# Final RMSNorm of a transformer layer: the last multiplies of the second half-rows on GpSimd instead of VectorE

## The chip, the core and the metric

The kernel runs on one core of a Trainium2 chip. A core has five engines with a queue each, worked off in order: TensorE (PE in the profile; its weight loads are PEld), VectorE (DVE), ScalarE (ACT), GpSimd (POOL) and SyncE (SP), which here issues all DMAs. They wait for each other through semaphores. The metric is the device time of one execution in microseconds, the median of the runs shown.

## The reference

One encoder layer over two batches with the same weights, 1024 and 512 rows of width 1024, then a last norm. What matters here is the end of it:

```python
def _rmsnorm(x, g):
    xf = x.astype(jnp.float32)
    y = xf * lax.rsqrt(jnp.mean(xf * xf, axis=-1, keepdims=True) + EPS)
    return (y * g.astype(jnp.float32)).astype(x.dtype)
...
    h = _rmsnorm(x, g_ffn)
    x = x + (jax.nn.silu(h @ w_ffn_gate) * (h @ w_ffn_up)) @ w_ffn_down
...
    return _rmsnorm(x, g_final)
```

## The kernel before

The 1536 rows are 12 tiles of 128 rows (t = 0 to 11), in two groups of six: g = 0 holds tiles 0 to 5, g = 1 tiles 6 to 11. The mixers run first, up to about 750 us. Then the feed-forward part loops over group, eleven slices p of the hidden width, and w = 0 (gate) or 1 (up). Each (g, p, w) is one `ffn_set`: seven products of 12 matmuls each on TensorE into three PSUM tiles psX, psY and psZ (products 0, 2, 4 and 6 use psX, 1 uses psY, 3 and 5 use psZ). A product that adds on to a PSUM tile waits until ScalarE has copied the sum so far out of it (`cp`, L1091). Every operand is a float32 split in a high and a low part, by a cast on ScalarE (L981) and a subtraction on VectorE (L982). After the gate set of the next slice, `down` multiplies the activations with the down weights into psd (L1156), and VectorE adds psd to the tile's row x2[t] (L1158), in the order 1, 3, 5, 0, 2, 4 within a group.

The last norm of a tile stands in two functions. `fin_ss` takes a buffer `out` (yo in the profile), squares the two halves of x2[t] into it on ScalarE with the row sums as a by-product (L1129), and makes the row's factor r on GpSimd in three instructions on 128x1 values: L1131, L1132 and the power of -0.5, L1133. `fin_y` multiplies: each half of the row is one instruction on VectorE (L1142), (x2 times r) times gF, 128x512, and then one DMA of 256 KB from SP (L1143). Here x2, yo and the gain gF all lie in SBUF.

This happens in two places. Tiles 0 to 5 are finished in the first gate set of g = 1, while its matmuls run; this is called the middle stage below, 1350 to 1400 us. Tiles 6 to 11 are finished in the last `down`, the end stage, from 1837 us on. The buffers yo come from the pool `wr` of four buffers of 4 KB per partition, which also holds the raw gate and up weights; so a yo, or a weight load, can take a buffer only when the output DMAs of the yo before it have landed. The sums of squares sq0 and sq1 have one buffer each, so the squares of the next tile wait for L1131 and L1132 of this one.

Matmuls keep the order in which they are written. On the other engines a scheduler sets the order of the queues, and which free buffer a tile takes, from its own cost model; so an edit in one place can change the queues of all four around it.

Of the kernel before, what the change touches and what calls it, by code (L numbers as in the profile page):

```python
# [13 lines left out]
ALU = mybir.AluOpType  # L14
# [787 lines left out]
def of_phase(tc, hp, x, catT, g_ffn, wg, wu, wd, g_fin, y, ident, before, hc, x2d):  # L802

    nc = tc.nc
    V, A, G, PE = nc.vector, nc.scalar, nc.gpsimd, nc.tensor
# [6 lines left out]
    x2 = {i: xr_p.tile([128, D], F32, tag=f"x{i}", name=f"x2_{i}") for i in range(2)}  # L812
# [309 lines left out]
    def fin_ss(t, keep=1):  # L1122
        out = wr.tile([128, D], F32, tag="raw", name="yo")
        sq = [small.tile([128, 1], F32, tag=f"sq{j}", bufs=1, name=f"sq{j}") for j in range(2)]
        ss = small.tile([128, 1], F32, tag="ss", name="ss")
        r = small.tile([128, 1], F32, tag="rf", bufs=4, name="rs")
        for j in range(2):
            js = slice(j * 512, (j + 1) * 512)
            A.activation(out[:, js], x2[t][:, js], AF.Square, accum_out=sq[j])  # L1129
            if j == 0:  # L1130
                G.tensor_scalar(ss, sq[0], 1.0, EPS * D, op0=ALU.mult, op1=ALU.add)  # L1131
        G.tensor_scalar(ss, sq[1], ss, 1.0 / D, op0=ALU.add, op1=ALU.mult)  # L1132
        G.tensor_tensor(r, ss, mh, op=ALU.pow)  # L1133
        fin.append((t, out, r))
        if len(fin) > keep:
            fin_y()

    def fin_y():
        t, out, r = fin.pop(0)
        for j in range(2):  # L1140
            js = slice(j * 512, (j + 1) * 512)
            V.scalar_tensor_tensor(out[:, js], x2[t][:, js], r, gF[0][:, js], op0=ALU.mult, op1=ALU.mult)  # L1142
            nc.sync.dma_start(y[t * 128:(t + 1) * 128, js], out[:, js])  # L1143

    def down(g, p):
# [20 lines left out]
    gF = [None]  # L1166
    LAST = 2 * NP - 1
    ends = (1, 3, 5, 0, 2, 4)

    def slots(n):  # L1170
        g, p, w = seq[n]
        z = [[] for _ in range(7)]
        if n == 0:
            z[0].append(lambda: o_tr(10))
            z[1].append(lambda: o_tr(11))
            z[2] += [lambda: fetch(1), lambda: fetch(2)]
        for i in range(4):
            z[i + 2 if n == 0 else i + 1 if n == LAST + 1 else i].append(lambda i=i: load_a(n + 1, i))
        if w == 1:
            for i in range(2):  # L1180
                z[i if n == len(seq) - 1 else 2 * i + 2].append(lambda i=i: load_d(p, i))
        if n == LAST:
            for ci in range(6):
                z[ci + 1].append(lambda ci=ci: load_sum(1, ci))
        if n == LAST + 1:
            z[2] += [load_gf, lambda: down(0, NP - 1)]
            for i, o in enumerate(ends):
                z[3 + i // 2].append(lambda o=o: fin_ss(o))
            z[6].append(fin_y)
        if n == LAST + 2:  # L1190
            for i, o in enumerate(ends):
                z[i].append(lambda o=o: reload(o))
        return z
# [16 lines left out]
    while fin:  # L1210
        fin_y()
# [121 lines left out]
```

## Time and profile before

| | |
|---|---|
| median of three runs | 1869.37 us (1869.08 to 1870.72) |
| the profiled execution | 1866.71 us |
| its span, first to last instruction | 1864.9 us |
| TensorE busy, share of the span | 98% |
| VectorE busy | 64% |
| ScalarE busy | 46% |
| GpSimd busy | 12% |
| mean granted TensorE clock | 0.997 |

The profile is of one execution; its span is 1.8 us shorter than its device time, and that is 2.7 us under the median. Busy shares are of the whole span; a stage of 50 us has its own.

### The profile page before, as it was taken

What the parts mean: (1) busy time and instruction counts of PE and PEld (TensorE: products, weight loads), DVE (VectorE), ACT (ScalarE), POOL (GpSimd) and SP (SyncE); (2) the same over time, 40 slices, a digit from 0 to 9 for tenths busy, and PEclk for the clock granted to TensorE, in tenths of its full rate; (3) what the DMA queues carried; (4) which work ended last, traced back from release to release, by engine and by line L of the source; (5) the groups of instructions that cost most, each with busy time, mean ns of one, the idle gap of its engine ahead of it and who ended that gap; (6) DMA issues with size and microseconds to landing.
All of it is one profiled execution on the core that took longest, in us unless ns stands there. A gap on an engine that the chain in (4) does not pass through costs nothing.

```text
span 1864.9 us, 28927 instructions
## 1 busy us (share of the span) xinstructions
PE 1822.6 (98%) x10734; PEld 1647.4 (88%) x10734; DVE 1196.0 (64%) x2389; ACT 853.0 (46%) x1882; POOL 215.9 (12%) x425
## 2 busy tenths in 40 slices
PE   8999999999999999998999999999999999999997
PEld 7889898898788878888999999999899999999996
DVE  6754555556756574548666666666887666666655
ACT  7764555556666663425333333333453333333332
POOL 4322212122322221000000000000010000000001
PEclk9999999999999999999999999999999999999999
DMA  7422022132222254366222222222462222222202
GB/s 251 133 88 88 19 69 60 58 102 83 76 84 76 61 175 141 97 183 220 70 76 69 68 72 75 69 68 68 132 226 94 69 68 68 69 68 68 69 23 91
DMA packets 113581, 174.67 MB, mean 94 GB/s; under 512 B 11017, under 2 KB 79497, under 8 KB 113441
## 3 DMA queue, kind: packets, MB, share of 16 engines
q1 hardware_dynamic: 113440, 172.83, 29.7%
q8 instruction: 84, 1.38, 0.3%
q14 instruction: 57, 0.46, 0.1%
HBM read 144.69 MB, written 28.05 MB: 93 GB/s over the span
## 4 chain that ended last, share of the span: by engine, by line
PE 76%; issue 8%; DVE 5%; DMA 5%; ACT 4%; POOL 1%; SPq 0%; POOLq 0%; DVEq 0%; ACTq 0%
PE psd L1156 18%; PE psX L1067 18%; PE pj L717 17%; PE psZ L1067 9%; PE psY L1067 4%; PE ptr L402 1%; DMA wraw<-in_w_in 1%; DMA bq<-hc 1%; PE pso L832 1%; PE psc L373 1%; PE psc L377 1%; PE pgl L541 1%; DVE wl L217 1%; ACT wh L216 1%; PE pv L473 1%
## 5 line engine op out<-in xcount | busy, mean ns | idle before, releaser
L717 PE MATMUL pj<-wh,hh 128*128 128x384 f32 (+1 forms) x768 | 284.4, 370 | 0.7 <-ACT wh L216 0.7
L717 PE MATMUL pj<-wl,hh 128*128 128x384 f32 (+1 forms) x768 | 260.6, 339 | 0.2 <-DVE wl L217 0.2
L717 PE MATMUL pj<-wh,hl 128*128 128x384 f32 (+1 forms) x768 | 260.4, 339 | 0.1
L1158 DVE TENSOR_TENSOR x<-psd,x 128x512 f32<-128x512 f32 x264 | 181.3, 689 | 111.1 <-PE psd L1156 111.0
L1156 PE MATMUL psd<-dh,ah 128*128 128x512 f32 x528 | 205.8, 390 | 1.4 <-DVE x L1158 1.4
L1156 PE MATMUL psd<-dl,ah 128*128 128x512 f32 x528 | 206.0, 390 | 0.1
L1156 PE MATMUL psd<-dh,al 128*128 128x512 f32 x528 | 206.0, 390 | 0.0
L981 ACT CAST dh<-wdr 128x1024 fp32r<-128x1024 f32 x44 | 46.4, 1055 | 306.6 <-PE psd L1156 295.9
L982 DVE TENSOR_TENSOR fl<-raw,fh 128x1024 fp32r<-128x1024 f32 x132 | 161.0, 1221 | 39.5 <-ACT fh L981 39.4
L981 ACT CAST fh<-raw 128x1024 fp32r<-128x1024 f32 x132 | 138.7, 1052 | 99.4 <-PE psX L1067 52.5
L717 PEld LDWEIGHTS pj<-wh,hh 128*128 128x128 f32 x768 | 145.2, 189 | 23.0 <-issue 14.8
L717 PEld LDWEIGHTS pj<-wl,hh 128*128 128x128 f32 x768 | 145.5, 189 | 2.0 <-DVE wl L217 1.0
L717 PEld LDWEIGHTS pj<-wh,hl 128*128 128x128 f32 x768 | 144.6, 188 | 0.7 <-DVE hl L177 0.4
L1131 POOL TENSOR_SCALAR ss<-sq 128x1 f32<-128x1 f32 x12 | 4.6, 382 | 990.9 <-ACT yo L1129 990.9
L1156 PEld LDWEIGHTS psd<-dh,ah 128*128 128x128 f32 x528 | 99.1, 188 | 22.5 <-DVE x L1158 2.3
L1156 PEld LDWEIGHTS psd<-dh,al 128*128 128x128 f32 x528 | 99.1, 188 | 20.9 <-DVE al L982 0.3
L1156 PEld LDWEIGHTS psd<-dl,ah 128*128 128x128 f32 x528 | 99.1, 188 | 20.6 <-DVE dl L982 0.5
L217 DVE SCALAR_TENSOR_TENSOR wl<-wraw,gm,wh 128x384 fp32r<-128x384 f32 (+1 forms) x128 | 79.7, 644 | 19.1 <-ACT wh L216 18.4
L362 POOL TENSOR_SCALAR sc<-sc,mx 128x512 f32<-128x512 f32 x96 | 66.5, 695 | 178.6 <-DVE mx L361 164.7
L216 ACT ACTIVATE wh<-wraw,gm 128x384 fp32r<-128x384 f32 (+1 forms) x128 | 75.8, 618 | 21.8 <-DMA wraw<-in_w_in 19.6
L360 ACT ACTIVATE sc<-sc,mx 128x512 f32<-128x512 f32 x96 | 68.8, 717 | 23.8 <-DVE mx L359 22.3
L1091 ACT COPY s<-psX 128x384 f32<-128x384 f32 x88 | 41.8, 475 | 48.3 <-PE psX L1067 48.3
(282 smaller groups left out, 4426.5 us busy)
## 6 DMA issues: line engine op xcount, KB each, us to landing
raw<-in_w_gate SPq DMA_DIRECT2D x44, 512.0 KB, 3.8
raw<-in_w_up SPq DMA_DIRECT2D x44, 512.0 KB, 3.7
wdr<-in_w_down SPq DMA_DIRECT2D x44, 512.0 KB, 4.0
wraw<-in_w_in SPq DMA_DIRECT2D x112, 192.0 KB, 2.5
bq<-hc SPq DMA_DIRECT2D x18, 384.0 KB, 3.6
hc<-hst SPq DMA_DIRECT2D x24, 256.0 KB, 5.0
out_y<-yo SPq DMA_DIRECT2D x24, 256.0 KB, 2.0
craw<-catT SPq DMA_DIRECT2D x11, 512.0 KB, 3.8
```

The lines of the kernel that those rows point to most:

```text
L216: A.activation(h[:, :n], r[:, :n], AF.Copy, scale=gm[:, k:k + 1])
L217: V.scalar_tensor_tensor(l[:, :n], r[:, :n], gm[:, k:k + 1], f32(h)[:, :n], op0=ALU.mult, op1=ALU.subtract)
L360: A.activation(sc[:, :w], sc[:, :w], AF.Exp, bias=nm, scale=0.125, accum_out=l)
L362: G.tensor_scalar(sc[:, :w], sc[:, :w], rl, 1.0, op0=ALU.mult, op1=ALU.mult)
L373: PE.matmul(ps[h][:, 0:256], lhsT=qf[r, 128 * t:128 * t + 128], rhs=strided(kf[r, 32 * t:32 * t + 1], (32, 2), (288, 4), (1, 32)), start=T ...
L717: PE.matmul(ps[:, :cols], lhsT=l_[:, k, :], rhs=r_[:, :cols], start=(k == 0 and i == 0), stop=(k == 7 and i == 2))
L981: A.copy(h, r)
L982: V.tensor_tensor(l, r, f32(h), op=ALU.subtract)
L1067: PE.matmul(ps, lhsT=a_[:, sl], rhs=b_[kk // 2][:, kk % 2], start=(first and kk == 0 and j == 0), stop=(kk == 3 and j == 2), skip_group_ch ...
L1091: A.copy(s, ps)
L1156: PE.matmul(ps, lhsT=a_[:, sl], rhs=b_[:, js], start=(i == 0 and q == 0), stop=(i == 1 and q == 2))
L1158: V.tensor_tensor(xs, ps, xs, op=ALU.add)
```

## The change

In `fin_y`, the second half of each row (j = 1) goes to GpSimd as two instructions, x2 times r into yo and yo times gF in place, for all tiles but t = 10, the last one in the order of the end stage. The first half of each row, and both halves of tile 10, stay one instruction on VectorE. The DMAs stay on SP.

```diff
         for j in range(2):
             js = slice(j * 512, (j + 1) * 512)
-            V.scalar_tensor_tensor(out[:, js], x2[t][:, js], r, gF[0][:, js], op0=ALU.mult, op1=ALU.mult)
+            if j and t != 6 + ends[-1]:
+                G.tensor_scalar(out[:, js], x2[t][:, js], r, 1.0, op0=ALU.mult, op1=ALU.mult)
+                G.tensor_tensor(out[:, js], out[:, js], gF[0][:, js], op=ALU.mult)
+            else:
+                V.scalar_tensor_tensor(out[:, js], x2[t][:, js], r, gF[0][:, js], op0=ALU.mult, op1=ALU.mult)
             nc.sync.dma_start(y[t * 128:(t + 1) * 128, js], out[:, js])
```

The new lines are L1143 and L1144; VectorE's multiply becomes L1146, and later lines move by four (L1156 is L1160, L1158 is L1162). `ends` is (1, 3, 5, 0, 2, 4).

The scheduler's order moves with it. First GpSimd in the end stage, tiles 8 and 10 (x2_8 is tile 8; ss and rs are the small values, numbers are those of buffers). Before:

```order
L1131 TENSOR_SCALAR ss_18770<-sq0_18768 128x1
L1132 TENSOR_SCALAR ss_18770<-sq1_18769,ss_18770 128x1
L1133 TENSOR_TENSOR rs_18771<-ss_18770,mh2_9258 128x1
L1131 TENSOR_SCALAR ss_18800<-sq0_18798 128x1
L1132 TENSOR_SCALAR ss_18800<-sq1_18799,ss_18800 128x1
L1133 TENSOR_TENSOR rs_18801<-ss_18800,mh2_9258 128x1
```

And now:

```order
L1131 TENSOR_SCALAR ss_18778<-sq0_18776 128x1
L1132 TENSOR_SCALAR ss_18778<-sq1_18777,ss_18778 128x1
L1133 TENSOR_TENSOR rs_18779<-ss_18778,mh2_9258 128x1
L1143 TENSOR_SCALAR yo_18775<-x2_8_14861,rs_18779 128x512
L1144 TENSOR_TENSOR yo_18775<-yo_18775,gF_18643 128x512
L1131 TENSOR_SCALAR ss_18809<-sq0_18807 128x1
L1132 TENSOR_SCALAR ss_18809<-sq1_18808,ss_18809 128x1
L1133 TENSOR_TENSOR rs_18810<-ss_18809,mh2_9258 128x1
```

So the two large multiplies of a tile stand ahead of the next tile's three small instructions. The same holds for every tile of both stages but one (in the middle, tile 0's L1131 slips between the two multiplies of tile 5).

Then ScalarE in the middle stage, around the copies out of psX and psZ (yo_14655 is tile 0's buffer, yo_14684 tile 2's and yo_14698 tile 4's; the names DMAHW are the semaphores of DMAs). Before:

```order
L1091 COPY s_14749<-psX_14734 128x384 [waits PE_49]
L1129 ACTIVATE yo_14655,sq0_14656<-x2_0_8985 128x512 [waits DMAHW3_49,DMAHW4_49,DVE_49,Pool_49]
L1129 ACTIVATE yo_14655,sq1_14657<-x2_0_8985 128x512 [waits Pool_49]
L1129 ACTIVATE yo_14684,sq0_14685<-x2_2_9261 128x512 [waits DMAHW5_49,DMAHW6_49,DVE_49,Pool_49]
L1129 ACTIVATE yo_14684,sq1_14686<-x2_2_9261 128x512 [waits Pool_49]
L1091 COPY s_14797<-psX_14734 128x384 [waits PE_49]
L981 CAST ah_14771<-s_14749 128x384 [waits DVE_49]
L1091 COPY s_14823<-psZ_14736 128x384 [waits PE_49]
L1129 ACTIVATE yo_14698,sq0_14699<-x2_4_9278 128x512 [waits DMAHW2_49,DMAHW1_49,Pool_49]
L1129 ACTIVATE yo_14698,sq1_14700<-x2_4_9278 128x512 [waits Pool_49]
```

And now (yo_14687 is tile 2's, yo_14702 tile 4's):

```order
L1091 COPY s_14755<-psX_14740 128x384 [waits PE_49]
L1129 ACTIVATE yo_14687,sq0_14688<-x2_2_9261 128x512 [waits DMAHW6_49,DVE_49,DMAHW7_49,Activation_49,Pool_49]
L1129 ACTIVATE yo_14687,sq1_14689<-x2_2_9261 128x512 [waits Pool_49]
L1129 ACTIVATE yo_14702,sq0_14703<-x2_4_9278 128x512 [waits DMAHW0_49,DMAHW1_49,DVE_49,Pool_49]
L1129 ACTIVATE yo_14702,sq1_14704<-x2_4_9278 128x512 [waits Pool_49]
L981 CAST ah_14777<-s_14755 128x384 [waits DVE_49]
L1091 COPY s_14803<-psX_14740 128x384 [waits PE_49]
L981 CAST fh_14805<-raw_14420 128x1024 [waits DVE_49]
L1091 COPY s_14829<-psZ_14742 128x384 [waits PE_49]
```

The squares of tile 4 now stand ahead of the second copy out of psX and of the copy out of psZ. Read with the whole program, the DMAs waited for are the outputs of the tile that had the buffer: tile 3's squares wait for the outputs of tile 1 (as before), tile 5's for those of tile 3, tile 2's for those of tile 5, and tile 4's for those of tile 0; tile 0's wait for none. Before, tile 5's waited for none, tile 0's for tile 3, tile 2's for tile 5, tile 4's for tile 0.

## Rows read from the trace of the kernel before

**Rows 1.** Page, part 1: busy us, share of the span, instructions, by engine.

```profile
PE 1822.6 (98%) x10734; PEld 1647.4 (88%) x10734; DVE 1196.0 (64%) x2389; ACT 853.0 (46%) x1882; POOL 215.9 (12%) x425
```

**Rows 2.** All waits of PE, 1300 to 1866: total us, times, longest.

```profile
PE psX L1067 <- ACT s L1091: 1.5, 1, 1.5
PE psd L1156 <- DVE x L1158: 1.4, 2, 1.0
PE psZ L1067 <- ACT s L1091: 0.5, 1, 0.5
```

**Rows 3.** Chain that ended last, 1336 to 1440: start us, us, what.

```profile
1358.33 0.67 DVE yo L1142
1359.02 2.43 DMA out_y<-yo
...
1361.79 1.33 ACT yo L1129 x4
...
1367.87 2.60 DMA out_y<-yo
...
1370.58 1.35 ACT yo L1129 x4
...
1372.57 0.56 POOL rs L1133
...
1375.49 0.47 ACT s L1091
...
1378.30 1.43 DVE yo L1142 x2
...
1380.18 5.38 DMA raw<-in_w_up
```

**Rows 4.** Timeline, end stage, TensorE, VectorE and GpSimd: start us, us, engine, line, operation.

```profile
1853.94 0.39 PE L1156 MATMUL psd<-dh,al 128*128 128x512 f32 x1
...
1857.80 0.68 DVE L1158 TENSOR_TENSOR x<-psd,x 128x512 f32<-128x512 f32 x1
...
1860.40 1.41 DVE L1142 SCALAR_TENSOR_TENSOR yo<-x,rs,gF 128x512 f32<-128x512 f32 x2 [1.26 <-POOL rs L1133]
...
1842.80 0.55 POOL L1133 TENSOR_TENSOR rs<-ss,mh 128x1 f32<-128x1 f32 x1
...
1859.47 0.26 POOL L1132 TENSOR_SCALAR ss<-sq,ss 128x1 f32<-128x1 f32 x1 [1.54 <-ACT yo L1129]
1859.82 0.55 POOL L1133 TENSOR_TENSOR rs<-ss,mh 128x1 f32<-128x1 f32 x1
```

**Rows 5.** Groups of GpSimd: count, busy us, mean ns, idle before.

```profile
L362 POOL TENSOR_SCALAR sc<-sc,mx 128x512 f32<-128x512 f32 x96 | 66.5, 695 | 178.6 <-DVE mx L361 164.7 <-DVE mx L359 13.1
...
L582 POOL TENSOR_TENSOR gr<-gr,zt 128x512 f32<-128x512 f32 x12 | 15.4, 1285 | 42.1 <-ACT zt L581 42.1
```

**Rows 6.** Timeline where GpSimd and VectorE overlap; L217's durations, min/median/max ns.

```profile
1841.22 0.19 POOL L1131 TENSOR_SCALAR ss<-sq 128x1 f32<-128x1 f32 x1 [462.96 <-ACT yo L1129]
...
1854.10 0.57 POOL L1131 TENSOR_SCALAR ss<-sq 128x1 f32<-128x1 f32 x1 [0.27 <-ACT yo L1129]
...
1853.86 0.75 DVE L1142 SCALAR_TENSOR_TENSOR yo<-x,rs,gF 128x512 f32<-128x512 f32 x1 [0.66 <-POOL rs L1133]
...
55.37 1.29 POOL L255 TENSOR_TENSOR lat<-zt,lat 128x512 fp32r<-128x512 f32 x1 [0.68 <-PE pj L717]
...
55.46 1.62 DVE L217 SCALAR_TENSOR_TENSOR wl<-wraw,gm,wh 128x384 fp32r<-128x384 f32 x1
...
L217 DVE SCALAR_TENSOR_TENSOR wl<-wraw,gm,wh x128: 596/616/1618, 5.5 to 654.9; 128x384 fp32r<-128x384 f32 x112, 128x416 fp32r<-128x416 f32 x16
```

**Rows 7.** Timeline, middle stage, GpSimd and TensorE.

```profile
1352.47 0.55 POOL L1133 TENSOR_TENSOR rs<-ss,mh 128x1 f32<-128x1 f32 x1
...
1373.28 0.33 PE L1067 MATMUL psX<-b4h,fh 128*128 128x384 f32 x1
```

**Rows 8.** Page, part 6: DMA issues, KB each, median us from issue to landing.

```profile
out_y<-yo SPq DMA_DIRECT2D x24, 256.0 KB, 2.0
```

## The prediction

> **What bounds the kernel now.** First the busy shares: TensorE works 98% of the span, VectorE 64%, GpSimd 12% [rows 1]. So nothing counts but where TensorE waits, and what follows its last matmul. From 1300 us on it waits four times, 3.4 us in all [rows 2]; the chain of waits then tells why.
>
> *Middle stage.* Between 1354 and 1398 us the chain that ended last runs through the very instructions that are moved [rows 3]: VectorE's second multiply of tile 1 ends at 1359.0, its output DMA lands 2.43 us later, only then have tile 3's squares a buffer (1361.79). The same stands again at 1367.87 and 1370.58, and at 1378.30 the multiplies of tile 4 hold back its outputs, and behind these on SP the weight load at 1380.18. Whatever lengthens a tile's way from r to its landed outputs lengthens this chain. Two of TensorE's waits hang on it: 0.5 us for the copy out of psZ and 1.5 us for one out of psX that stood behind that late load.
>
> *End stage.* The last matmul starts at 1853.94 and takes 0.39 us, but VectorE takes up its result only at 1857.80, 3.4 us late, and the last multiplies start at 1860.40 [rows 4]. The factor r of the first tile is done at 1843.35 (1842.80 + 0.55), that of the last at 1860.37: five tiles at 3.40 us each, where TensorE needs 12 matmuls of 0.227 = 2.72 us. VectorE does two additions and two multiplies per tile and waits for r in between. So this stage is worth 3.4 us at most, if the multiplies cost nothing elsewhere.
>
> **The change part by part.**
>
> *VectorE is relieved* of 11 multiplies of 0.75 us (the pair is 1.41, so 0.67 each in a row), 7.4 us in all. None of it counts unless VectorE is what a stage waits for; with r later, it waits for r.
>
> *GpSimd gets 22 instructions.* The nearest rows have the same form and shape: a multiply by a per-row factor and a constant, 0.695 us, and a product of two 128x512 tiles in place, 1.285 us [rows 5]. So 1.98 us stand for 0.67. They stand in GpSimd's queue ahead of the next tile's L1131 to L1133, so the next r waits for them.
>
> *The two engines block each other.* [Rows 6] show it both ways. L1131 takes 0.19 us alone, but 0.57 when it starts inside VectorE's multiply: it ends at 1854.67, 0.06 after that multiply (1854.61). And L217, three operands of which two are tiles in SBUF as in L1142, takes 0.616 us at the median, but 1.62 when it starts 0.09 us after a GpSimd product: it ends 0.42 after that one (57.08 against 56.66). So whoever comes second waits for the other's end, and then saves about 0.13 to 0.19 of its own time. On r both want to start: VectorE follows r by 0.03 us (1860.40 against 1860.37), GpSimd itself by 0.09 (1859.82 against 1859.73, the end of L1132) [rows 4]. So VectorE's multiply of the first half goes first, GpSimd's first one ends 0.69 - 0.13 = 0.56 after it, and the second, 0.07 later, takes 1.29. From r to GpSimd's end that is 0.03 + 0.75 + 0.56 + 0.07 + 1.29 = 2.70 us; without any blocking 0.09 + 0.69 + 0.07 + 1.29 = 2.14. I take 2.70.
>
> By the Trainium skill, page "SBUF — State Buffer", section "Who interferes with whom", a VectorE instruction with two SBUF inputs and a GpSimd instruction that reads SBUF shut each other out for the whole instruction, whichever starts first. Taken at its word, GpSimd's first multiply would end 0.69 after VectorE's and not 0.56, and the end stage below would come out 5 x 0.13 = 0.65 us longer; the rows decide for 0.56.
>
> *End stage, sum.* A tile on GpSimd is L1131 0.19, a step of about 0.06, L1132 0.26, a step of 0.09, L1133 0.55 (together 1.15, [rows 4, 6]), and 2.70: 3.85 us, over the 3.40 of before. VectorE has 2 x 0.69 + 0.75 = 2.1 us of work in it and is covered, ScalarE too. So r of tile 10 ends at 1843.35 + 5 x 3.85 = 1862.6 instead of 1860.37: **+2.2 us**. Without blocking the tile is 3.29 and the stage gains 0.55. Tile 10 itself is unchanged behind r. The psd buffers (four) are freed late, but TensorE just gets them in time.
>
> *Middle stage.* r of tile 1 ends at 1353.02 (1352.47 + 0.55) [rows 7]. GpSimd runs at once and is done at 1355.2; VectorE's half, which stands behind additions in its queue, then waits for GpSimd until about 1355.8. The outputs land at about 1358.0 (2.2 us, between the 2.0 at the median of all issues [rows 8] and 2.43), so tile 3's squares start 3.8 us earlier than before: a gain, since the second half no longer stands behind VectorE's other work. From there every tile costs: squares' start to r 2.55 (1370.58 to 1373.13, [rows 3]), r to the end on GpSimd 2.70, landing 2.3 (2.0 to 2.60, [rows 3, 8]): 7.55 us. Tile 3's outputs land at 1365.55. Tile 5's squares wait for them, tile 0's follow directly. r of tile 5 is at 1368.1; its multiplies end at 1371.05 (0.25 for tile 0's L1131 in between) and land at 1373.35, when tile 2's squares start. GpSimd goes on with tile 0: r at 1372.0, multiplies to 1374.7, landed at 1377.0; tile 4's squares run to 1378.35. All that time ScalarE's queue stands still ahead of the cast ah and the copy out of psX, 0.47 us [rows 3] and about as much for the cast: copied at 1379.2. TensorE's fifth product waits for this copy; before, it started at 1373.28 [rows 7]. That is +5.9 us.
>
> What stands behind it: VectorE's addition L1085 that frees psX for the seventh product stands behind tile 4's multiply and a 1.2 us split that GpSimd's products block in turn; 0 to 2.5 us, I take 1.2. The weight load: after tile 0 GpSimd does tiles 2 and 4, 1.15 + 2.70 each, to 1382.4, against 1379.73 before, so the load is issued 2.7 us later. TensorE is by then later than that, so the old wait of 1.5 us for it goes, and the 0.5 at psZ too: -2.0. VectorE also works on splits with two SBUF inputs all through this stage, and each that starts ahead of a GpSimd product costs the chain up to 1.2 us; over five tiles 0 to 6 us, I take 1.4, nearer to the low end because VectorE's queue itself waits for r in many of them. Middle: 5.9 + 1.2 - 2.0 + 1.4 = **+6.5 us**. [Rows 2] hold every wait to the end, and none of it is in the slices that follow, so what is lost here stays lost.
>
> Sum: 2.2 + 6.5 = +8.7. Against the profiled execution 1866.71 + 8.7 = 1875.4; against the median, 2.7 us above it, 1869.4 + 8.7, rounded to **1878.0**.
>
> **The rivals.**
>
> *No blocking that counts.* If the new instructions pass beside VectorE's, a tile costs 2.55 + 2.14 + 2.3 = 7.0 us. Then the copy out of psX comes at about 1377.0, +3.7; less the 2.0 of waits, and less 0.55 at the end: +1.2, 1870.6. Against it stand both stretched instructions of [rows 6]. Chance 0.13.
>
> *The copies are covered.* If tile 4's squares find their buffer in time (the landings are the least certain term), the middle stage comes out even and only the end stage loses: +2.2, 1871.6. For it speaks tile 3's early start. Chance 0.12.
>
> *Faster.* One mechanism: VectorE was the late engine in the end stage, and with half its multiplies gone it keeps TensorE's pace. The last addition then starts at 1854.4 instead of 1857.80 and 3.4 us are saved; if the early start of tile 3 also clears the two waits of 2.0 us, the time is 1864.0. It decides at GpSimd's time per tile: at 3.40 us it turns, at 2.72 it is all gained. The bare sum of the rows, 1.15 + 2.14 = 3.29, is barely on this side, the blocked one is not. Chance 0.04. The Trainium skill, page "Perfetto Trace Analysis", section "Optimizing Scalar/DVE Operations", says that with a saturated VectorE moving some work to ScalarE or even GpSimd may make sense, and warns that GpSimd shares a port with it; the gain would be this rival, the warning is the blocking above.
>
> *Much slower.* VectorE's splits get in ahead of GpSimd at nearly every tile of the middle stage: the 1.4 becomes 6, and 1.2 becomes 2.5: +14.6, 1884. Chance 0.09.
>
> **How the numbers follow.** The forecast, 1874 to 1882 by its own bounds (GpSimd blocked for 0.56 or 0.69, landing 2.0 to 2.6, the two chosen terms), has 0.62. The range reaches down to the two rivals at 1870.6 and 1871.6 and up to 1884: 1870.5 to 1884. About 0.2%, 3.7 us, is what a measurement can tell from no change here. Faster by more: 0.04. Within: the two middle rivals, less the 0.03 by which they reach above 1873.1, 0.22. Slower: 0.62 + 0.09 + 0.03 = 0.74.
>
> **What would show it.** In the profile after: GpSimd's L1143 at 1.25 to 1.35 us (0.69 if nothing blocks) and L1144 at 1.29; the factors r 3.85 us apart in the end stage, the last multiply 2.2 us later against the last matmul; a wait of 4 to 6 us of TensorE at a psX product in the middle stage with a copy L1091 as its releaser, and ScalarE waiting for output DMAs ahead of it; the old 1.5 us wait gone. The prediction is wrong if the r's stand 3.3 us or less apart, or if TensorE waits no more than before between 1350 and 1400.

## The result and the profile after

The changed kernel takes 1882.10 us at the median (1879.99 to 1883.64, six runs) against 1868.78 (1866.39 to 1870.72) for the kernel before on the same chip: a ratio of 1.0065, with a 95% interval of 1.0055 to 1.0074, so 10.3 to 13.8 us slower, 12.1 by the ratio. The forecast was 1878.0, in a range of 1870.5 to 1884.0.

The profiled execution has a span of 1880.9 us. Its busy shares [rows 1] are nearly the same: GpSimd has 29 us more, VectorE only 3 less, although eleven multiplies left it: the time for which it is held inside an instruction counts as busy (its first multiply in the middle stage reads 1.73 us instead of 0.75).

```profile
PE 1828.2 (97%) x10734; PEld 1651.3 (88%) x10734; DVE 1192.7 (63%) x2378; ACT 854.6 (45%) x1882; POOL 245.1 (13%) x447
```

All waits of TensorE from 1300 us on, which answer to [rows 2] (total us, times, longest), and behind them the largest of ScalarE's between 1345 and 1420 us:

```profile
PE psX L1067 <- ACT s L1091: 8.8, 3, 5.5
PE psd L1160 <- DVE x L1162: 2.6, 3, 1.4
PE psX L1067 <- DVE gt L1077: 0.3, 1, 0.3
PE psZ L1067 <- ACT s L1091: 0.2, 1, 0.2
...
ACT yo L1129 <- DMA out_y<-yo: 11.7, 4, 3.5
```

The same wait of ScalarE in the kernel before:

```profile
ACT yo L1129 <- DMA out_y<-yo: 1.4, 1, 1.4
```

The chain that ended last in the middle stage answers to [rows 3] (start us, us, what):

```profile
1359.03 2.59 DMA out_y<-yo
...
1361.72 1.35 ACT yo L1129 x4
...
1364.23 1.27 POOL yo L1143
...
1365.57 2.15 POOL yo L1144
1367.73 2.42 DMA out_y<-yo
...
1378.23 1.60 POOL yo L1144
1379.84 2.42 DMA out_y<-yo
...
1382.36 1.35 ACT yo L1129 x4
...
1390.61 5.34 DMA raw<-in_w_up
...
1396.03 1.06 ACT fh L981
```

Squares, r, two GpSimd multiplies, landing, squares again; and at its end the weight load that stood on SyncE's queue behind the last outputs. In the end stage, one tile on GpSimd, and VectorE's last multiplies (timeline; [rows 4, 6] of before):

```profile
1868.04 0.55 POOL L1133 TENSOR_TENSOR rs<-ss,mh 128x1 f32<-128x1 f32 x1
1868.68 1.25 POOL L1143 TENSOR_SCALAR yo<-x,rs 128x512 f32<-128x512 f32 x1
1870.02 1.27 POOL L1144 TENSOR_TENSOR yo<-yo,gF 128x512 f32<-128x512 f32 x1
1871.26 0.19 POOL L1131 TENSOR_SCALAR ss<-sq 128x1 f32<-128x1 f32 x1
1871.54 0.27 POOL L1132 TENSOR_SCALAR ss<-sq,ss 128x1 f32<-128x1 f32 x1
1871.89 0.55 POOL L1133 TENSOR_TENSOR rs<-ss,mh 128x1 f32<-128x1 f32 x1
...
1876.32 1.42 DVE L1146 SCALAR_TENSOR_TENSOR yo<-x,rs,gF 128x512 f32<-128x512 f32 x2 [2.50 <-POOL rs L1133]
```

r stands 3.85 us behind r here, 3.87 at the mean of the five, and GpSimd never pauses.

Profiled executions differ before 1300 us, where nothing was changed (the psd products there start between 1298.5 and 1305.9). So traces are compared by stage. **Middle** below is the time from the first psd matmul of the last `down` of the first group (1338.16 before, 1339.92 after) to that of the first `down` of the second group (1396.66, 1410.63); the six tiles are finished between the two. **End** is the time from the first r of tiles 6 to 11 to the last. Three kernels with the same middle program (before, `e1_end`, `e6_psum`) have 57.8 to 58.9 us there, so differences of about 1 us there are chance.

| kernel | ratio to before | 95% | middle, us | end, us |
|---|---|---|---|---|
| before | 1 | | 58.50 | 17.02 |
| after | 1.0065 | 1.0055 to 1.0074 | 70.71 | 19.35 |
| e1_end | 1.0015 | 1.0006 to 1.0023 | 57.84 | 19.32 |
| e2_mid | 1.0057 | 1.0044 to 1.0069 | 69.57 | 16.99 |
| e6_psum | 1.0009 | 1.0001 to 1.0018 | 58.86 | 16.57 |
| e4_inplace_pool | 1.0051 | 1.0038 to 1.0064 | 68.21 | 17.00 |
| e5_inplace | 0.9988 | 0.9979 to 0.9996 | 56.60 | 17.02 |
| e7_queue | 1.0107 | 1.0092 to 1.0123 | 77.19 | 17.04 |
| e8_free_squares | 1.0059 | 1.0045 to 1.0073 | 68.88 | 16.99 |
| e11_batch | 1.0071 | 1.0057 to 1.0085 | 70.21 | 16.69 |
| e12_no_gain | 1.0014 | 1.0005 to 1.0023 | 61.61 | 17.00 |
| e3_fill | 1.0080 | 1.0067 to 1.0093 | 70.84 | 19.34 |
| e3b_fill45 | 1.0100 | 1.0087 to 1.0114 | 75.33 | 19.32 |
| e9_best | 0.9988 | 0.9980 to 0.9997 | 56.61 | 16.39 |

### The profile page after: what moved, and what is told of

It reads as the page before. It is cut to its first block, busy times and chain, and to the rows that moved or that the text cites. A ratio compares the mean times of both kernels' runs of the same rounds, so it can differ in the third digit from the quotient of the medians.

```text
span 1880.9 us, 28961 instructions
## 1 busy us (share of the span) xinstructions
PE 1828.2 (97%) x10734; PEld 1651.3 (88%) x10734; DVE 1192.7 (63%) x2378; ACT 854.6 (45%) x1882; POOL 245.1 (13%) x447
## 3 DMA queue, kind: packets, MB, share of 16 engines
q8 instruction: 84, 1.38, 0.3%
## 4 chain that ended last, share of the span: by engine, by line
PE 76%; issue 7%; DMA 5%; ACT 5%; DVE 4%; POOL 2%; SPq 0%; POOLq 0%; DVEq 0%; ACTq 0%
PE psX L1067 18%; PE psd L1160 18%; PE pj L717 17%; PE psZ L1067 9%; PE psY L1067 4%; DMA bq<-hc 1%; PE ptr L402 1%; DMA wraw<-in_w_in 1%; PE pso L832 1%; PE psc L373 1%; PE psc L377 1%; DVE wl L217 1%; PE pgl L541 1%; PE pv L473 1%; ACT wh L216 1%
## 5 line engine op out<-in xcount | busy, mean ns | idle before, releaser
L1162 DVE TENSOR_TENSOR x<-psd,x 128x512 f32<-128x512 f32 x264 | 181.0, 688 | 113.2 <-PE psd L1160 113.2
L1160 PE MATMUL psd<-dh,ah 128*128 128x512 f32 x528 | 205.9, 390 | 2.6 <-DVE x L1162 2.6
L1160 PE MATMUL psd<-dh,al 128*128 128x512 f32 x528 | 206.0, 390 | 0.0
L1160 PE MATMUL psd<-dl,ah 128*128 128x512 f32 x528 | 205.8, 390 | 0.0
L1131 POOL TENSOR_SCALAR ss<-sq 128x1 f32<-128x1 f32 x12 | 2.9, 238 | 984.8 <-ACT yo L1129 984.8
L1160 PEld LDWEIGHTS psd<-dh,ah 128*128 128x128 f32 x528 | 99.1, 188 | 24.0 <-DVE x L1162 3.9
L1160 PEld LDWEIGHTS psd<-dh,al 128*128 128x128 f32 x528 | 99.1, 188 | 21.0 <-DVE al L982 0.3
L1160 PEld LDWEIGHTS psd<-dl,ah 128*128 128x128 f32 x528 | 99.1, 188 | 20.1
L217 DVE SCALAR_TENSOR_TENSOR wl<-wraw,gm,wh 128x384 fp32r<-128x384 f32 (+1 forms) x128 | 79.5, 642 | 19.2 <-ACT wh L216 18.0
L216 ACT ACTIVATE wh<-wraw,gm 128x384 fp32r<-128x384 f32 (+1 forms) x128 | 75.7, 618 | 22.0 <-DMA wraw<-in_w_in 21.5
L1067 PE MATMUL psX<-b2h,fh 128*128 128x384 f32 x176 | 59.5, 338 | 6.8 <-ACT fh L981 3.5
```

The costliest lines, as they stand in the source:

```text
L216: A.activation(h[:, :n], r[:, :n], AF.Copy, scale=gm[:, k:k + 1])
L217: V.scalar_tensor_tensor(l[:, :n], r[:, :n], gm[:, k:k + 1], f32(h)[:, :n], op0=ALU.mult, op1=ALU.subtract)
L1067: PE.matmul(ps, lhsT=a_[:, sl], rhs=b_[kk // 2][:, kk % 2], start=(first and kk == 0 and j == 0), stop=(kk == 3 and j == 2), skip_group_ch ...
L1160: PE.matmul(ps, lhsT=a_[:, sl], rhs=b_[:, js], start=(i == 0 and q == 0), stop=(i == 1 and q == 2))
L1162: V.tensor_tensor(xs, ps, xs, op=ALU.add)
```

## The experiments

### One stage at a time: e1_end and e2_mid

```diff
-            if j and t != 6 + ends[-1]:
+            if j and t >= 6 and t != 6 + ends[-1]:     (e1_end)
+            if j and t < 6:                            (e2_mid)
```

> The move for the last six tiles alone (6 to 11, the very last stays on VectorE), the middle stage as before. Theory: the two stages lose separately; here GpSimd's time for one tile rises from 3.40 to about 3.87 us with the waiting of the two engines for each other, so the last five r's stand 3.87 apart and the kernel takes 2.3 us more (ratio about 1.0012); TensorE's waits between 1340 and 1420 us are those of before (1.5 for psX, none of over 3). Rival, the two stages are coupled (a middle stage that ends late is what makes the last stage late): here the end costs nothing, within 0.5 us of before.

> The move for the first six tiles alone (0 to 5), the end stage as before. Theory: the whole middle loss of the changed kernel, about 10.4 us (ratio about 1.0056): TensorE waits some 5.5 us for the fifth product of a psX set, released by ScalarE's copy, and ScalarE before it waits for out_y DMAs; the r's of the end stage are 3.4 us apart again. Rival, the middle loss belongs to the late bq loads that the profile of the changed kernel showed by chance: then under 5 us.

Both as the theory had it, up to the size of one wait. The end stage alone costs 0.15% (r's 3.86 us apart), the middle alone 0.57%. TensorE's waits at psX in `e2_mid`, between 1345 and 1420 us:

```profile
PE psX L1067 <- ACT s L1091: 7.4, 3, 4.0
```

The longest is 4.0 and not 5.5, because here the matmuls behind the third product's wait already ran at the lower clock (see the runs on the clock below). Together the two stages cost 0.72%, the change 0.65%: the stages add up, and four fifths of the loss are the middle's.

### What GpSimd's 3.87 us are made of: e6_psum

```diff
+            gP[0] = psA.tile([128, 512], F32, tag="a", name="gP")
+            A.copy(gP[0], gF[0][:, 0:512])
...
+                gain = gP[0] if t >= 6 and j == 0 else gF[0][:, js]
```

This stands on `e1_end`.

> As the move for the last six tiles alone, but the gain's first half is copied once to PSUM by ScalarE, and VectorE's multiplies of the first halves of these tiles read it there, so that each reads only one SBUF tile. Theory: GpSimd's 3.87 us for one tile consists of some 3.3 us of its own work and 0.57 us of waiting while VectorE's multiply with two SBUF operands runs; the r's stand about 3.3 apart, and the kernel is 0.5 us shorter than before instead of 2.3 longer. Rival, the time is GpSimd's own: 3.87 apart again, +2.3 us.

GpSimd's timeline in the end stage:

```profile
1855.27 0.70 POOL L1143 TENSOR_SCALAR yo<-x,rs 128x512 f32<-128x512 f32 x1
1856.05 1.30 POOL L1144 TENSOR_TENSOR yo<-yo,gF 128x512 f32<-128x512 f32 x1
```

0.70 and not 1.25: with one SBUF operand on VectorE nothing blocks, the r's are 3.31 apart, and the stage is 2.8 us shorter than in `e1_end`. So 0.55 of GpSimd's 3.87 us is waiting for VectorE's multiply. By the Trainium skill, page "SBUF — State Buffer", section "Who interferes with whom", a VectorE instruction with at most one SBUF input, outside its two-port modes, does not contend with GpSimd; this run agrees (0.70 against 1.25). The kernel was expected to be 0.5 us faster than before and came out 0.09% slower (0.01 to 0.18%, about 1.7 us): by the trace ScalarE's copy of the gain waited 2.8 us for its load with casts for the last psd products behind it, some 0.55 us on TensorE. That is not all of the difference; the rest stays open.

### The first theory, the buffers: e4_inplace_pool and e5_inplace

```diff
+        if t < 6:
+            out = x2[t]
```

In `e4_inplace_pool` this stands on `e2_mid`, in `e5_inplace` on the kernel before. The tile yo then holds squares only.

> The move for the first six tiles alone, with the results of these tiles written over x2 in place; the tile yo then holds only squares, is free as soon as ScalarE has read them out, and neither ScalarE's next squares nor the weight loads into the same buffers wait for the output DMA. Theory A (the loss comes over the buffers: multiply, output DMA, buffer free, squares, copies behind them): the 5.5 us wait of TensorE goes, at most 4 of the 11 us of the middle stage remain, ratio at most 1.002. Rival B (the loss comes over SyncE's queue, where the loads of raw stand in order behind output DMAs that wait for GpSimd's multiplies): 6 us or more remain, since the multiplies are as late as before.

> The kernel before, with the results of the first six tiles written over x2 in place, all multiplies on VectorE. Theory A: ScalarE's waits for output DMAs go, TensorE's old 2.0 us (1.5 and 0.5) for ScalarE's copies too: 1 to 2 us shorter than before (ratio 0.999 to 0.9995). Rival, the reloads of x for tiles 6 to 11 now have to wait for the output DMAs that read x2 and come too late, or VectorE's multiplies are the limit: no gain, 0 to +1 us.

Theory A fell: 9.7 of 11 us stayed with no square waiting for a DMA. All of ScalarE's squares and the copies between them stand in the same order in these two kernels, so the pair tells what the move costs with the buffers out of play: 68.21 against 56.60, 11.6 us, as much as with them (69.57 - 58.50 = 11.1). The order is not the same everywhere: on VectorE the multiplies stand elsewhere among the splits, and a weight load that SyncE's queue has between outputs in `e5_inplace` stands behind them in `e4_inplace_pool`. TensorE's one long wait has moved to psZ; the rows of `e4_inplace_pool`, first a wait of TensorE, then ScalarE's timeline, show who holds it:

```profile
PE psZ L1067 <- ACT s L1091: 7.3, 1, 7.3
```

```profile
1367.02 0.63 ACT L1129 ACTIVATE yo<-x 128x512 f32<-128x512 f32 x1 [2.76 <-POOL ss L1131]
...
1370.14 0.46 ACT L1091 COPY s<-psZ 128x384 f32<-128x384 f32 x1
```

The copy stands behind squares of six tiles, and these wait for GpSimd to have read the sums of the tile before (one buffer for each sum). `e5_inplace` itself is 0.12% faster than before (0.04 to 0.21%), a little more than its theory had: between the two `down`s TensorE no longer waits at all.

### SyncE's queue: e7_queue

```diff
-            nc.sync.dma_start(y[t * 128:(t + 1) * 128, js], out[:, js])
+            (nc.gpsimd if j and t < 6 else nc.sync).dma_start(y[t * 128:(t + 1) * 128, js], out[:, js])
```

This stands on `e2_mid`.

> The move for the first six tiles alone, but GpSimd itself issues the output DMAs of the second halves that it has multiplied, so that SyncE's queue holds none that waits for GpSimd; the buffers stay as in the changed kernel. Rival B (SyncE's queue): the raw loads are issued 6 us earlier or more, and at most 4 of the 11 us remain. Theory A (the buffers): ScalarE's squares still wait for DMAs that read yo, TensorE's wait of 4 to 5.5 us stays, and 6 us or more remain (ratio 1.003 or more).

Rival B fell, and the time is far over what theory A needs: 7.6 us more than `e2_mid`. Its chain in the middle stage, then a wait of SyncE's queue and the landings of GpSimd's outputs (median us from issue, 1350 to 1402 us), say why:

```profile
1361.03 4.55 DMA out_y<-yo
...
1385.72 0.29 issue
1386.01 0.05 POOL out_y L1147
1386.06 0.61 issue
```

```profile
SPq L1147 <- DVE yo L1146: 30.6, 6, 8.3
...
out_y<-yo POOLq DMA_DIRECT2D x6, 256.0 KB, 2.9
```

The first output issued by GpSimd landed after 4.55 us and the six after 2.9 at the median (2.0 for the twelve that SyncE issued in `e2_mid`), each issue took GpSimd nearly 1 us with its gaps, and SyncE's queue waited anyway, for VectorE's first halves, which wait for the same r. So the run gave GpSimd more to do and doesn't tell the queue from the buffers; that SyncE's queue is the path stays open by it.

### The squares' wait taken away: e8_free_squares

```diff
-        sq = [small.tile([128, 1], F32, tag=f"sq{j}", bufs=1, name=f"sq{j}") for j in range(2)]
+        if not sqs:
+            sqs.extend(small.tile([128, 8], F32, tag=f"sq{j}", bufs=1, name=f"sq{j}") for j in range(2))
+        sq = [q[:, t % 6:t % 6 + 1] for q in sqs]
```

This stands on `e4_inplace_pool`.

> The kernel of the move for the first six tiles with results in place (it took 9.7 us more than before although no square waited for an output DMA; there TensorE stood 7.3 us for a copy that ScalarE had behind squares, and these waited for GpSimd to read the sums of the tile before). Here the sums of the six tiles have six columns of their own, so that no square waits for GpSimd; the order of the instructions is the same on every engine. Theory A2: ScalarE's in-order copies behind squares that wait for GpSimd, by whichever wait, are what costs; the 7.3 us wait goes and the middle stage comes within 3 us of the one with VectorE's multiplies in place (from the psd products of the set before to those of this set 56.6 to 59.6 us instead of 68.2; ratio 1.0005 or less). Rival C: VectorE's own multiplies wait 2.4 to 3.1 us for each r behind GpSimd's multiplies, with splits and gates of the next products behind them; that stays, TensorE waits for those instead, and the stage keeps 64 us or more (ratio 1.003 or more).

Theory A2 fell, rival C held: 68.88 us. The squares now run through (the copy out of psZ at 1361.7 instead of 1370.1), and TensorE waits as long, for VectorE. A wait of TensorE, then VectorE's timeline:

```profile
PE psX L1067 <- DVE gt L1077: 7.1, 1, 7.1
```

```profile
1367.40 0.75 DVE L1150 SCALAR_TENSOR_TENSOR x<-x,rs,gF 128x512 f32<-128x512 f32 x1 [3.09 <-POOL rs L1135]
1370.99 0.75 DVE L1150 SCALAR_TENSOR_TENSOR x<-x,rs,gF 128x512 f32<-128x512 f32 x1 [2.84 <-POOL rs L1135]
1371.66 0.55 DVE L1077 TENSOR_TENSOR gt<-psX,s 128x384 f32<-128x384 f32 x1
```

The gate gt for which TensorE waits is two multiplies behind, and each waits for an r that stands behind GpSimd's multiplies.

### The r's ahead of the multiplies: e11_batch

```diff
+        if len(fin) == 6:
...
+            for k in range(6):
+                G.tensor_tensor(r[:, k:k + 1], ss[:, k:k + 1], mh, op=ALU.pow)
+            fin[:] = [(t, out, r[:, k:k + 1]) for k, (t, out, _) in enumerate(fin)]
+            for _ in range(6):
+                fin_y()
```

This stands on `e8_free_squares`; the edit is shown in part.

> The kernel of the run before last (first six tiles in place, sums of their own, second halves still multiplied by GpSimd), but GpSimd makes the six r's in one go, after the last square and ahead of all its multiplies. GpSimd has the same multiplies to do as there. Theory C2: what costs in the middle stage is that each r stands behind the multiplies of the tile before it on GpSimd, 3.4 to 4.3 us apart, and that VectorE or ScalarE, which wait for it, hold the products' work behind them; with the r's 0.6 us apart VectorE waits once, TensorE's 7 us wait shrinks under 2.5, and from the psd products of the set before to those of this set it takes 57 to 60.5 us instead of 68.9 (ratio 1.001 or less). Rival D: GpSimd's long multiplies cost by themselves (late output DMAs, loads behind them on SyncE's queue, VectorE's instructions held up beside them): 64 us or more stay (ratio 1.003 or more).

Rival D held: 70.21 us. TensorE's 7 us wait did go; the products run on until 1379 us. Then it waits 4.2 us at psZ and, in the next set, 4.8 at psX. The loss has moved on once more (timelines of GpSimd, VectorE, SyncE's queue and ScalarE):

```profile
1368.86 2.30 POOL L1161 TENSOR_SCALAR x<-x,r 128x512 f32<-128x512 f32 x2
...
1383.58 3.79 POOL L1162 TENSOR_TENSOR x<-x,gF 128x512 f32<-128x512 f32 x2
...
1386.16 2.30 DVE L982 TENSOR_TENSOR fl<-raw,fh 128x1024 fp32r<-128x1024 f32 x1
...
1366.22 21.51 SPq L1165 DMA_DIRECT2D out_y<-x  x12
...
1397.02 1.04 ACT L981 CAST dh<-wdr 128x1024 fp32r<-128x1024 f32 x1 [8.37 <-DMA wdr<-in_w_down]
```

GpSimd's twelve multiplies take from 1368.9 to 1387.4 in one row. Beside them VectorE's splits take 2.30 instead of 1.22, and the loads stand on SyncE's queue behind twelve outputs for 21.5 us, so that ScalarE waits 8.4 us for weights.

### Less work for GpSimd: e12_no_gain

```diff
                 G.tensor_scalar(out[:, js], x2[t][:, js], r, 1.0, op0=ALU.mult, op1=ALU.mult)
-                G.tensor_tensor(out[:, js], out[:, js], gF[0][:, js], op=ALU.mult)
```

This stands on `e2_mid`.

> The move for the first six tiles alone, in the form of the changed kernel (buffers, queue and r's as there), but GpSimd's product with the gain (1.27 to 2.15 us each) is left out of their second halves, so that GpSimd only multiplies by r (0.70 to 1.77 us). Three waits have been taken away one at a time, and each time another took its place and 10 to 13 us stayed. Theory E: the loss is the time that GpSimd's work for the six tiles takes, whichever wait hands it on; with GpSimd's time for one tile down by a third (from 3.9 to about 2.5 us) at most 4 of the 11 us of the middle stage stay (from the psd products of the set before to those of this set 62.5 us or less, ratio at most 1.0025). Rival F: it is the move as such (instructions placed in another order on ScalarE and VectorE, output DMAs that wait for another engine): 8 us or more stay (ratio 1.004 or more).

The numbers of theory E held: 61.61 us, so 3.1 of 11 us stay with a third of GpSimd's time for a tile gone. Waits of TensorE and of ScalarE between 1345 and 1420 us:

```profile
PE psX L1067 <- ACT s L1091: 2.6, 2, 2.3
PE psX L1067 <- DVE s L1085: 2.1, 1, 2.1
...
ACT yo L1129 <- DMA out_y<-yo: 6.5, 4, 2.0
```

The squares still wait four times for output DMAs, but for 6.5 us and not 11.6 as in `e2_mid`, and TensorE's longest wait at psX for ScalarE is 2.3 and not 4.0. From the r of tile 1 to the squares of tile 4 it takes 21.2 us instead of 26.0. On that stretch ScalarE has the same order but for one cast, and 4.8 of the 8 us that came back are the shorter chain of squares, multiply and landing. The other 3 lie behind it, where the scheduler's order is not that of `e2_mid`: casts change places on ScalarE, and a load of down weights stands ahead of the up weights on SyncE's queue. VectorE's order of splits and multiplies differs on both stretches. So rival F, the order, is weakened and not excluded.

### The clock: e3_fill and e3b_fill45

After the wait of 5.5 us TensorE's matmuls started 0.33 us apart instead of 0.173. Rows of after, first TensorE's timeline, then the busy times by window (us, PE, PEld, DVE, ACT and POOL busy, then the granted clock as a share of full, DMA share, GB/s):

```profile
1384.53 0.69 PE L1067 MATMUL psX<-b4h,fh 128*128 128x384 f32 x1 [5.55 <-ACT s L1091]
```

```profile
1384.53:1389.81 5.28, 5.28 (x17) 5.28 (x17) 3.54 (x5) 2.31 (x3) 4.92 (x6) 0.50 0.44 168
1389.81:1396.00 6.19, 6.19 (x37) 6.19 (x37) 3.94 (x6) 0.52 (x1) 0.34 (x1) 1.00 0.78 220
```

0.50 is the lower of the clock's two levels, 1.2 GHz; sixteen matmuls at it cost 16 x (0.330 - 0.173) = 2.5 us. The two runs keep TensorE busy in that wait:

```diff
+            if n == 2 * NP + 1 and i == 4:
+                fill = psB.tile([128, 512], F32, tag="b", name="fill")
+                for _ in range(NFILL):        (20, then 45)
+                    PE.transpose(fill[:, 0:128], ident, ident)
```

> The changed kernel with 20 dummy transposes of a 128x128 identity on TensorE, put just ahead of the product for which TensorE stood still for 5.5 us (they take about 4 us there, and nobody reads them). Theory: the 16 matmuls after that stall took 0.32 us each and not 0.17 because the granted clock fell to the lower level after TensorE had stood still; with TensorE busy in the stall they take 0.17 again and the kernel is some 2.4 us shorter than the changed one (about 1879.5 against 1882). Rival, the clock falls for another reason (or the time is taken by a wait for the late raw load behind it, 1.2 us and more): no gain, 0 to +1 us against the changed one.

> The changed kernel with 45 dummy transposes (0.118 us each, 5.3 us) in place of 20 in TensorE's long wait: 20 left 3.3 us of it idle and the clock fell again. Theory now: TensorE's wait shrinks to under 1.5 us and the matmuls behind it take 0.17 us each, but the kernel is not shorter (within 1 us of the changed one, about 1882), because the first psX product of the next set waits for a raw load that lands at the same time as before; the psd products of the first set of the second group start some 70.8 us after those of the set before, as in the changed kernel. Rival, the slow matmuls are on the path: 2.4 us shorter.

The 20 took only 2.35 us; 3.3 us of the wait were left and eleven matmuls ran at the lower clock again, so that run told little. With 45 the clock stays up; rows of `e3b_fill45`, TensorE's timeline and a window:

```profile
1383.82 0.44 PE L1068 MATMUL psX<-b4h,fh 128*128 128x384 f32 x1 [0.64 <-ACT s L1092]
...
1402.87 0.69 PE L1068 MATMUL psX<-b2h,fh 128*128 128x384 f32 x1 [7.50 <-ACT s L1092]
```

```profile
1383.80:1388.80 5.00, 4.44 (x24) 4.12 (x24) 3.24 (x4) 2.35 (x3) 4.64 (x6) 1.00 0.43 162
```

That it is not shorter was expected; that it is 4.6 us longer in the middle was not. TensorE gets through the set sooner and then waits 7.5 us at the next one's third product (the second into psX), whose copy stands behind casts that wait for late loads; behind that wait twelve matmuls run at the lower clock once more (0.52 granted from 1402.87 to 1406.76). So the lower clock is real, and in the chain of the changed kernel the stage ends on the load and not on it. These two runs fit that and don't prove it: the order on ScalarE differs here too (a cast of dh stands ahead of that copy and waits 7.4 us), and where the extra 4.6 us come from was not settled.

### A version faster than both: e9_best

```diff
+            if j and t >= 6 and t != 6 + ends[-1]:
+                A.activation(out[:, js], x2[t][:, js], AF.Copy, scale=r)
+                G.tensor_tensor(out[:, js], out[:, js], gF[0][:, js], op=ALU.mult)
```

Beside this, the gain's first half in PSUM as in `e6_psum` (its copy placed later), sums of their own, and VectorE's multiplies in place for tiles 0 to 5.

> A version put together from the runs: first six tiles in place with all multiplies on VectorE and sums of their own (as the kernel that was 0.12% faster than before); last six tiles with the gain's first half in PSUM for VectorE, the second half scaled by r on ScalarE, and only the product with the gain on GpSimd (1.29 us). Theory: GpSimd's time for one tile is then about 2.65 us, under TensorE's 2.73 for its psd products, so the r's of the end stand 2.7 to 2.8 apart instead of 3.40, and from the first r to the last 13.7 us instead of 17.0; with the middle's 1.9 us the kernel takes some 5 us less than before (ratio about 0.9973). Rival, ScalarE's scalings hold up the squares behind them, or the multiplies of VectorE and GpSimd still block each other: 3.1 or more apart, ratio 0.9982 or more.

It is 0.12% faster than before (0.03 to 0.20%), less than half of what was expected and no more than `e5_inplace` alone. The middle gives its 1.9 us. In the end the r's are 3.28 apart and not 2.7, since GpSimd now pauses 0.84 us inside each tile, until ScalarE's scaling (L1150) is done; the timeline names other releasers for some of these pauses, but the multiply starts 0.08 us after the scaling in each:

```profile
1852.09 0.55 POOL L1135 TENSOR_TENSOR rs<-ss,mh 128x1 f32<-128x1 f32 x1
...
1852.67 0.72 ACT L1150 ACTIVATE yo<-x,rs 128x512 f32<-128x512 f32 x1 [1.18 <-POOL rs L1135]
...
1853.47 1.27 POOL L1151 TENSOR_TENSOR yo<-yo,gF 128x512 f32<-128x512 f32 x1 [0.84 <-DMA out_y<-yo]
```

## Why the prediction was right or wrong, step by step

- **Blocking, 0.56 us a tile.** Right: L1143 took 1.25 us, L1144 1.26 to 1.29, and `e6_psum` shows the cause; the tile without blocking, 3.29 in the sum, is 3.31 there. Had GpSimd been held for its whole instruction, 0.69, L1143 would have read 1.38.
- **End stage, +2.2.** Right: 19.35 - 17.02 = +2.3, r's 3.87 apart against 3.85.
- **The fifth product, +5.9.** Right in place and releaser: TensorE's wait there is 5.55 us, and ScalarE waited for output DMAs ahead of the copy, as forecast. Counted as the prediction counts, from the stage's start (3.2 us later in this trace), the product starts 8.0 us later than before, where 5.9 and the 1.4 for splits were forecast. Of this 2.2 stood already at the third product, a wait of 2.0 us that the sum did not have. That the other 5.8 look like the 5.9 is partly luck.
- **Splits ahead of GpSimd, +1.4.** About right on the way to the fifth product and missing behind it. By GpSimd's timeline, against 1.25, 1.29 and the usual times of the small steps, its instructions were held 1.7 us longer for tiles 3, 5 and 0, and 2.6 longer for tiles 2 and 4 (L1143 up to 1.77, L1144 up to 2.14). The 2.6 reach TensorE by the load below.
- **L1085 and the seventh product, +1.2.** Didn't come: TensorE doesn't wait there. In four of the other runs it does, for 1.5 to 2.6 us (`e4_inplace_pool`, `e7_queue`, `e8_free_squares`, `e12_no_gain`).
- **The clock, not in the sum.** The matmuls behind the 5.55 us took 2.5 us longer by their rows. They stand in front of the late load, so it was not shown that the stage would have ended sooner without this.
- **Old waits gone, -2.0.** Half right: the 0.5 at psZ is gone, and so is the 1.5 at its product. But the load that the 1.5 stood for still holds TensorE, two products earlier.
- **The weight load, 2.7 us later and covered.** This is the step that failed. The load is issued at 1390.61 instead of 1380.18, which is 7.2 us later without the 3.2, behind the last multiply on GpSimd (done at 1390.2 and not at 1382.4 plus 3.2, which is 4.6 us late). It lands 5.34 us after, and the next set's third product, whose copy stands behind the cast of that load, waits 1.2 us:

```profile
1388.02 2.13 POOL L1144 TENSOR_TENSOR yo<-yo,gF 128x512 f32<-128x512 f32 x1
...
1398.85 0.44 PE L1067 MATMUL psX<-b2h,fh 128*128 128x384 f32 x1 [1.22 <-ACT s L1091]
```

The same product waits 3.5 and 7.5 us in the two runs that filled the wait ahead, with other orders on ScalarE. So the stage does not end on the wait that the sum priced, but on this one.
- **Middle in all.** 6.5 was forecast, and the first matmul behind the stage's last psd products stands 13.6 - 3.2 = 10.4 us later. The 3.9 us between lie in three places: 0.7 up to the fifth product (8.0 against 7.3), another 1.1 up to the seventh (9.8 against 8.0; the clock's 2.5 came where L1085's 1.2 was priced), and another 2.1 behind that, where the sum took 1.5 back and 0.6 more was lost to the late load and small waits.
- **The number.** 1882.1 is in the stated range, but just above 1874 to 1882, the forecast's own bounds. It is inside because the range reaches up to the rival "much slower".
- **The theory behind the middle term was too narrow.** It told the one path that ended last (multiply, landing, buffer, squares, copy). With that path out of the way (`e4_inplace_pool`) 9.7 us of the stage's loss stayed by way of the sums' buffers, without these (`e8_free_squares`) 10.4 by way of VectorE's waits for r, and without these (`e11_batch`) 11.7 by way of late loads and blocked splits. Only less GpSimd work brought most of the time back (`e12_no_gain`), or none (`e5_inplace`). So the runs point to GpSimd's time for a tile as the common cause. Two things keep this from being proved: the scheduler's order differs between the kernels of both comparisons, and no run freed SyncE's queue of outputs that wait for GpSimd without giving GpSimd more to do. How much each path would cost if all others were free was not measured.
- **Rivals.** "No blocking that counts" is excluded by 1.25 us, "the copies are covered" by the 5.5 us wait, "faster" by r's that stand 3.87 apart. "Much slower" had VectorE's splits as what grows, and the time came two thirds of the way to it: GpSimd was held 4.3 us longer and not 6, and part of it reached TensorE by the load, which this rival did not name.

## What to carry to other kernels

Work moved to an engine that was idle 88% of the time cost 0.65% here, because its result lies between two engines that work in order: count the whole time per tile on the new engine, with its own small steps and with what the blocking by the other engine adds, and compare it with the pace around it. Where that time was too long, taking away the wait that ended last did not help here; the next in-order queue handed it on, and what helped was a shorter time per tile. In such a sum follow the loads behind the moved step to their landing even where a longer wait stands ahead of them.

## What the runs showed of the hardware

- The granted clock fell to 0.50 behind the 5.55 us wait and stayed there for 5.28 us; behind 0.64 us of waiting after dummy transposes it stayed at 1.00. The third product's wait, 1.9 us in `e2_mid` and 2.0 in the changed kernel, was followed by twelve slow matmuls in the one (0.54 granted from 1375.79 to 1379.50) and by none in the other (1.00).
- Six outputs of 256 KB issued from GpSimd landed after 2.9 us at the median in the middle stage (the first after 4.55), against 2.0 for twelve from SyncE in `e2_mid`. Each issue took GpSimd 0.61 to 0.77 us.
- 45 transposes of 128x128 on TensorE took 5.08 us, 0.113 each.
